# Hybrid decoder step: cache tiles kept together in pairs on TensorE, batched norm sums, idle products in the norms

## The chip, the cores and the metric

The kernel runs on one NeuronCore of one Trainium2 chip. The metric is the device time of one execution in microseconds (us). Three runs of the kernel before took 1901.42, 1902.14 and 1903.34 us, median 1902.14 us. The profiled execution took 1903.54 us, of which 1901.8 us lie between its first and last instruction (the span).

## What is computed

Two layers of a decoder trunk for two request groups that share weights: one prompt of 256 tokens, and 8 samples of 4 tokens each, so 288 columns in all, 1024 channels. Per layer:

```python
h = rmsnorm(x);  proj = h @ w_in                 # one combined input projection
#  A. gated DeltaNet, 8 heads:  q, k = l2norm(q), l2norm(k);  chunked delta rule
#  B. dilated window attention, 3 groups x 4 heads; a sample reads cache_win{1,2,3}_k / _v
#  C. Mamba-2 SSD, 16 heads, gated, grouped RMSNorm
merged = g_dn*(o_dn @ w_br_dn) + g_dil*(o_dil @ w_br_dil) + g_ssm*(o_ssm @ w_br_ssm)
x = x + rmsnorm(merged @ w_out)                  # "mixpost"
x = x + rmsnorm(crossattn(rmsnorm(x)) @ w_mo)    # "mempost"; memory k, v from rmsnorm(mem)
x = x + rmsnorm(relu(rmsnorm(x) @ w_ff1)**2 @ w_ff2)   # "ffnpost"
```

All results are float32. The states of all three mixers are returned as well.

## The kernel before, in words

**Projections.** Activations lie transposed, as eight tiles of 128 channels x 288 columns. Each is split into a high and a low part (`xh`, `xl`), each weight too (`wh`, `wl`), so a 128 x 128 weight tile costs three matmuls of 288 columns into a bank `mmps` (or `mmx`). Weights come from `in_wst` in blocks of four tiles (256 KB, tile `wr`), ScalarE casts `wh`, VectorE subtracts to `wl`. There are 3600 weight tiles, 10,800 such matmuls.

**Background work.** The three mixers, apart from their projections, are Python generators (`spawn`, `step`). At every fourth weight tile, `w` calls `tick`, which advances two of them to their next `yield`. So the program text of the mixers is woven into that of the projections.

**Order on the engines.** The program text is not the final order. A planner at compile time lists each engine's instructions by when it believes their inputs and buffers are there. An instruction that it believes late is put behind later text that is ready. It sets the order once; on the chip each engine runs its list in order, and each instruction waits by semaphore. Buffers come from pools with a fixed number of slots (`N_A` = 50 activation tiles, `N_M` = 9 large tiles `M`, 5 PSUM banks `X`); a load waits until its tile has a slot.

**The cache work of the sample.** `dil_sample` (L1692 on) reads cache tiles of 512 KB (`kc`, from pool `M`) through `caches(name, n, depth=2)`, which loads two ahead. Per layer there are 4, 8 and 2 tiles of keys (`k1`, `k2`, `k3`) and 4, 2 and 8 of values (`v1`, `v3`, `v2`). `qk_cache` (L1667) multiplies key tiles into `sqk`, `pv_cache` (L1676) value tiles into `spo`; each matmul uses 32 of the array's columns, four heads side by side. A float32 matmul stands in the trace as two records, so a tile of values gives 16. `qk_cache` yields after every tile of `k1` and `k3` and every second one of `k2`, `pv_cache` after every second tile. The cross-attention (`cross_sample`, tiles `mqk`, `mpo`) uses the same two helpers with depth 5.

**Sums of squares.** `dn_mix` (L837) forms the norms of q and k per half of the heads: four squares of q on ScalarE, four (eight records of 288 columns) matmuls into `l2` (in the trace: `l`), then the same for k. `mem_norm` (L631) adds eight squares on VectorE (`gather`) and sums the result with four matmuls into `ss`; `ssm_gate` (L1501) adds two squares for each of four groups and sums with four matmuls into `yn`.

**Post-norms.** `postnorm` (L586) runs eight projections, sums the squares (`ss`), forms the factor on VectorE (`row`, nine dependent instructions ending with `rms`), spreads it with four matmuls (`bc`) and updates x, from which the next `xh`, `xl` come. For `mixpost` two pieces of other projection work (`fill`: columns of the memory's keys) stand around the spread; for `mempost` and `ffnpost` nothing does.

Of the kernel before, what the change touches and what calls it, by code (L numbers as in the profile page):

```python
# [10 lines left out]
BF16 = mybir.dt.bfloat16  # L11
I32 = mybir.dt.int32
AF = mybir.ActivationFunctionType
ALU = mybir.AluOpType
# [3 lines left out]
P = 128  # L18
# [8 lines left out]
NSTEP = 2  # L27
IDLE, IDLE2 = 1, 1
GATE = 3
HDV = 1  # L30
RAW, AHEAD = 6, 2
N_A, N_M = 50, 9
# [192 lines left out]
class Net:  # L225
    def __init__(self, ctx, tc, ins, outs, coff, nl):
        self.tc, self.nc = tc, tc.nc
        self.I, self.O, self.nl = ins, outs, nl
        self.coff, self.moff = coff
        pool = lambda name, bufs, **k: ctx.enter_context(tc.tile_pool(name=name, bufs=bufs, **k))  # L230
        self.cpool = pool("cpool", 1)
        self.pa = pool("pa", N_A)
        self.pm = pool("pm", N_M)
        self.pw = pool("pw", 3)
        self.psm = pool("psm", 2)
        self.pr = pool("pr", 1)
        self.mm = pool("mm", 3, space=PSUM)
        self.mx = pool("mx", 5, space=PSUM)
        self.pd = ctx.enter_context(tc.tile_pool(name="pd", bufs=2, space=bass.MemoryType.DRAM))
        self.cbi = self.zi = 0  # L240
        self.order, self.wt = [], {}
        self.nload = self.nsplit = 0
        self.gate, self.nstep, self.sqs = (0,), NSTEP, []
        self.bg, self.lazy, self.done = [], [], set()
        self.setup()


# [34 lines left out]


    def mmul(self, out, lhsT, rhs, start=True, stop=True):
        self.nc.tensor.matmul(out, lhsT, rhs, start=start, stop=stop)  # L285

    def tp(self, out, in_):
        self.nc.tensor.transpose(out, in_, self.ident)
# [85 lines left out]
    def setup(self):  # L374
        nc = self.nc
        self.prmt = {}
        cw = sum(w for _, w in self.coff.values())
        self.cst = self.cpool.tile([P, cw], F32, tag="cst", name="cst")
        self.xt = [self.A(nm="x") for _ in range(8)]
        self.params(0)  # L380
        for c in range(8):
            self.load(self.xt[c], self.I["x"][:, c, :])
            if c < RAW:
                self.load_weights(c)
            if c == 1:
                self.load(self.cst[:, 0:256], self.I["cst"][:, 0:256])
        self.ident, self.ones = self.C("ident"), self.C("ones")
        self.Z = [self.zeros([P, 1024], f"z{i}") for i in range(2)]
        self.CB = [self.zeros([P, 316], f"cb{i}") for i in range(4)]
        self.cmz = self.zeros([P, 2, 256], "cmz")  # L390
        self.St = {}
        for k, w in (("dst", T), ("sst", T + 128)):
            self.St[k] = self.cpool.tile([P, w], F32R, tag=k, name=k)
            nc.gpsimd.memset(self.St[k].bitcast(F32), 0.0)
        self.z3 = self.cpool.tile([P, 512], F32, tag="z3", name="z3")
        nc.vector.memset(self.z3, 0.0)
        self.tsd = self.cpool.tile([P, P], F32, tag="tsd", name="tsd")
        self.cp(self.tsd, self.z3[:, 0:128])
        self.tok0 = self.zeros([P, 3, 32], "tok0")
        self.mc = self.zeros([P, 8, 32], "mc")  # L400
        self.tT = self.zeros([P, 8, 128], "tT")
        self.t64 = self.zeros([P, 8, 64], "t64")
        self.gtok = self.zeros([P, 6, 3, 24], "gtok")
        self.l2t = self.cpool.tile([P, 3, 2, 4], F32, tag="l2t", name="l2t")
        nc.gpsimd.memset(self.l2t, 1.0)
# [133 lines left out]
                self.mmul(ps[32 * g:32 * g + 32, 0:w], self.ones[:, 0:32], sq[:, w * g:w * g + w],  # L539
                          i == 0, i == len(sqs) - 1)  # L540

    def gather(self, acc, sq, w=T):

        if acc is None:
            return sq
        self.tt(acc[:, 0:w], acc[:, 0:w], sq[:, 0:w], ALU.add)
        return acc

    def sums(self, ss):

        def after(k):
            if k == 7:
                self.sumsq(ss, self.sqs)
                self.sqs = []
        return after

    def row(self, ps, w=72):
        r = self.S(w, "rms")
# [27 lines left out]
    def postnorm(self, gname, wname, xs, each, eps=None, fill=None, part=None, k0=0):  # L586

        ss = self.X("ss")
        fs, sqs = [], [None]
        ps = self.projs([(wname, n * 128) for n in range(2)], xs) if k0 == 0 else []  # L590
        for n in range(8):
            b = ps[n] if n < len(ps) else self.proj(wname, n * 128, xs, k0)
            sq = self.A(nm="sq")
            if part is None:
                f = self.A(nm="f")
                last = self.act(sq, b[:, 0:T], AF.Square)
                self.ts(f, b[:, 0:T], self.prm(gname, n))
            else:
                f = part[n]
                self.tt(f, f, b[:, 0:T], ALU.add)  # L600
                last = self.act(sq, f, AF.Square)
                self.act(f, f, AF.Copy, scale=self.prm(gname, n))
            fs.append(f)
            if n < 6:
                sqs[0] = self.gather(sqs[0], sq)
            else:
                sqs.append(sq)
        self.gate = (self.nsplit + GATE, last)
        g0 = self.nsplit + GATE
        self.sumsq(ss, sqs)  # L610
        if eps is None:
            r = self.row(ss)
        else:
            v, r, y, t = self.S(72, "qv"), self.S(72, "rms"), self.S(72, "ry", I32), self.S(72, "rt")
            self.stt(v, ss[:, 0:72], 1.0 / 1024, eps, ALU.mult, ALU.add)
            self.last = self.rsqrt_of(r, v, y, t)
        self.gate = (g0, last, self.last)
        if fill:
            fill[0]()
        bc = self.spread(r)  # L620
        if fill:
            fill[1]()
        res = []
        each = each()
        for n in range(8):
            self.tt(fs[n], fs[n], bc[:, 0:T])
            self.tt(self.xt[n], self.xt[n], fs[n], ALU.add)
            res.append(each(n))
        return res


    def mem_norm(self):
# [2 lines left out]
            self.load(mem[i], self.I["mem"][:, 4 * i:4 * i + 4, :])  # L635
        for _ in range(4):
            yield
        acc = None
        for c in range(8):
            sq = self.A(nm="sq")  # L640
            self.act(sq[:, 0:256], mem[c // 4][:, c % 4], AF.Square)
            acc = self.gather(acc, sq, 256)
            if c % 2:
                yield
        yield
        yield
        ss = self.X("ss")
        self.sumsq(ss, [acc], w=64)
        r = self.row(ss, 64)
        yield  # L650
        yield
# [187 lines left out]
    def dn_mix(self, hf, q, k, v):  # L839
# [2 lines left out]
            yield  # L842

        l2 = self.X("l2")
        for i, src in enumerate((q, k)):
            sqs = [self.A(nm="sq") for _ in range(4)]
            for h in range(4):
                self.act(sqs[h], src[h], AF.Square)
                if h == 1:
                    yield  # L850
            yield 1
            for h in range(4):
                self.mmul(l2[32 * h:32 * h + 32, 0:T], self.C("zs")[:, 31 - i:63 - i], sqs[h], i == 0, i == 1)
        lr = self.A(nm="l2r")
        self.cp(lr, l2[:, 0:T])

# [643 lines left out]

    def ssm_gate(self, xs):  # L1501
        Y = self.Y
        accs = [None] * 4
        for t in range(8):
            z = self.gate_z(IN_OFF["ssz"] + t * 128, xs)
            self.need(f"ssm{t // 2}")
            self.stt(Y[t], Y[t], 0.5, z)
            sq = self.A(nm="sq")
            self.act(sq, Y[t], AF.Square)
            accs[t // 2] = self.gather(accs[t // 2], sq)  # L1510
        yn = self.X("yn")
        for g in range(4):
            self.mmul(yn[32 * g:32 * g + 32, 0:T], self.ones[:, 0:32], accs[g])
        self.ssmR = self.quad_rows(yn, 1.0 / 256)

    def ssm_out(self):
# [125 lines left out]
            self.cp(self.diag(z, h), ps[:, 32 * h:32 * h + 32].rearrange("p (b s) -> p b s", b=NB))  # L1642
        return z.rearrange("p (h b s) -> p h b s", h=4, b=NB)

    def caches(self, name, n, depth=2):

        l, buf = self.l, []

# [14 lines left out]
    def qk_cache(self, ps, qm, tiles, n, nk, per):  # L1663
        for i, t in enumerate(tiles):
            kv = t.rearrange("p (b h k) -> p b h k", b=per, h=4)
            for j in range(per):
                b = i * per + j  # L1667
                for h in range(4):
                    self.mmul(ps[32 * h:32 * h + 32, 0:nk], qm[:, h, b], kv[:, j, h], b == 0, b == NB - 1)
            if i % 2 or per > 1:  # L1670
                yield

    def pv_cache(self, po, tiles, n, prods, first=False, last=False):

        for i, vt in enumerate(tiles):
            pr = prods(i)  # L1676
            for j, (lh, o) in enumerate(pr):
                for h in range(4):
                    self.mmul(po[32 * h:32 * h + 32, 0:128], lh(h), vt[:, o + h * 128:o + h * 128 + 128],
                              first and i + j == 0, last and i == n - 1 and j == len(pr) - 1)  # L1680
            if i % 2:
                yield

    def dil_sample(self):
# [309 lines left out]

    def run(self):
        self.l = 0
        x0, n = [], AHEAD + 1
        with self.tc.manual_schedule(engines={mybir.EngineType.Activation, mybir.EngineType.DVE}):
            for c in range(n):
# [62 lines left out]
```

## Time and profile before

| | us |
|---|---|
| median of 3 runs | 1902.14 |
| the profiled execution | 1903.54 |
| its span | 1901.8 |
| TensorE (PE) busy in the span | 1848.5 (97%) |
| VectorE (DVE) busy | 1411.0 (74%) |
| ScalarE (ACT) busy | 1126.7 (59%) |
| GpSimd (POOL) busy | 305.0 (16%) |
| mean granted TensorE clock | 0.989 of full |

A matmul's duration in the trace holds its way through the array, so the records of a dense stream overlap. What a matmul costs in a stream is the distance between two starts: 0.13 us for 288 columns at full clock. What a visit of other work between two projection matmuls costs is read from ends: the end of the first projection matmul after it, less the end of the last before it, less 0.13 us.

### The profile page before, as it was taken

How to read it: one execution, taken by the hardware profiler on the slowest of the kernel's cores; microseconds unless marked ns; L12 is line 12 of the kernel's file. 1: busy time of each engine (PE TensorE's matmuls, PEld its weight loads, DVE VectorE, ACT ScalarE, POOL GpSimd, SP SyncE). 2: the span in 40 equal slices, each digit the busy share in tenths (PEclk: the TensorE clock that was granted, in tenths of full speed). 3: DMA queues.
4: the chain of work that ended last, by engine and by line, in shares of the span. 5: the costliest groups of instructions: out<-in, count | busy, mean ns of one | idle time of the engine just before them, and what ended most of it. 6: DMA issues, size and time to landing. Idle time of an engine off the chain costs nothing. (4 is left out here: it accounts for less than half of the span.)

```text
span 1901.8 us, 44052 instructions
## 1 busy us (share of the span) xinstructions
PE 1848.5 (97%) x16182; PEld 1726.9 (91%) x16182; DVE 1411.0 (74%) x3168; ACT 1126.7 (59%) x2735; POOL 305.0 (16%) x777
## 2 busy tenths in 40 slices
PE   8999999999999999999899999999999999999997
PEld 8998999988998988999899889989889999789997
DVE  6978767677978758766588785776788887587665
ACT  5666665655555556756466756656554555476563
POOL 3523212322000000000024222133210000000000
PEclk9999999999999999999999999999999999989999
DMA  7545436588554684766555453465875556747763
GB/s 254 174 143 170 118 115 199 161 286 270 188 170 143 208 279 129 242 206 201 153 150 182 123 182 106 142 191 158 303 247 191 172 165 208 246 139 238 212 192 99
DMA packets 184441, 354.49 MB, mean 186 GB/s; under 512 B 30688, under 2 KB 42144, under 8 KB 184224
## 3 DMA queue, kind: packets, MB, share of 16 engines
q1 hardware_dynamic: 176320, 326.44, 55.0%
q0 software_dynamic: 7904, 25.23, 3.9%
q8 instruction: 127, 2.08, 0.4%
q14 instruction: 90, 0.74, 0.1%
HBM read 316.54 MB, written 35.05 MB: 185 GB/s over the span
## 5 line engine op out<-in xcount | busy, mean ns | idle before, releaser
L293 ACT CAST wh<-wr 128x512 fp32r<-128x512 f32 x900 | 555.6, 620 | 563.4 <-PE mmps L285 473.4
L302 DVE TENSOR_TENSOR wl<-wr,wh 128x512 fp32r<-128x512 f32 x900 | 619.7, 692 | 286.3 <-ACT wh L293 273.6
L285 PE MATMUL mmps<-xh,wh 128*128 128x288 f32 x2400 | 728.2, 306 | 14.2 <-ACT wh L293 6.8
L285 PE MATMUL mmps<-xl,wh 128*128 128x288 f32 x2400 | 714.6, 298 | 0.0
L285 PE MATMUL mmps<-xh,wl 128*128 128x288 f32 x2400 | 712.8, 297 | 1.0 <-DVE wl L302 1.0
L285 PEld LDWEIGHTS mmps<-xh,wh 128*128 128x128 f32 x2400 | 453.4, 190 | 33.4 <-issue 12.4
L285 PEld LDWEIGHTS mmps<-xl,wh 128*128 128x128 f32 x2400 | 456.1, 190 | 9.3 <-issue 5.6
L285 PEld LDWEIGHTS mmps<-xh,wl 128*128 128x128 f32 x2400 | 454.7, 189 | 7.7 <-issue 3.8
L285 PE MATMUL mmps<-prs,wh 128*128 128x288 f32 x1280 | 262.8, 298 | 2.9 <-ACT prs L293 2.2
L285 PEld LDWEIGHTS mmps<-prs,wh 128*128 128x128 f32 x1280 | 206.2, 189 | 6.1 <-ACT prs L293 3.0
L285 PE MATMUL mmps<-prs,wl 128*128 128x288 f32 x640 | 189.0, 295 | 0.0
L311 DVE SCALAR_TENSOR_TENSOR cy<-cb,cwh,cy 128x312 f32<-128x312 f32 x240 | 129.4, 539 | 19.3 <-ACT cy L290 12.7
L285 PEld LDWEIGHTS mmps<-prs,wl 128*128 128x128 f32 x640 | 121.0, 189 | 0.0
L285 PE MATMUL mmps<-ph,wh 128*128 128x288 f32 x256 | 76.5, 299 | 0.0
L285 PE MATMUL mmps<-pl,wh 128*128 128x288 f32 x256 | 75.6, 295 | 0.0
L285 PE MATMUL mmps<-ph,wl 128*128 128x288 f32 x256 | 75.6, 295 | 0.0
L330 POOL DMA_DIRECT2D out_osd<-dnu x32 | 17.3, 541 | 346.4 <-DVE dnu L311 338.0
L299 POOL COPY cvp<-cb 128x3 f32<-128x3 f32 x80 | 30.2, 378 | 213.7 <-ACT cb L293 213.4
L290 ACT ACTIVATE ct<-cy 128x312 f32<-128x312 f32 x80 | 37.3, 466 | 37.4 <-DVE cy L311 33.5
L285 PEld LDWEIGHTS mmps<-ph,wh 128*128 128x128 f32 x256 | 48.1, 188 | 2.1 <-ACT b L293 0.8
L285 PEld LDWEIGHTS mmps<-pl,wh 128*128 128x128 f32 x256 | 48.2, 188 | 0.7 <-issue 0.4
L285 PEld LDWEIGHTS mmps<-ph,wl 128*128 128x128 f32 x256 | 48.1, 188 | 0.4 <-issue 0.4
(506 smaller groups left out, 2910.1 us busy)
## 6 DMA issues: line engine op xcount, KB each, us to landing
wr<-in_wst SPq DMA_DIRECT2D x900, 256.0 KB
kc<-in_k SPq DMA_DIRECT2D x28, 512.0 KB
kc<-in_v SPq DMA_DIRECT2D x28, 512.0 KB
dns<-in_dns SPq DMA_DIRECT2D x16, 512.0 KB
h<-in_h SPq DMA_DIRECT2D x16, 512.0 KB
out_oss<-h POOLq DMA_DIRECT2D x16, 512.0 KB, 3.9
kc<-in_km SPq DMA_DIRECT2D x16, 512.0 KB
kc<-in_vm SPq DMA_DIRECT2D x16, 512.0 KB
```

The source lines that it names most:

```text
L285: self.nc.tensor.matmul(out, lhsT, rhs, start=start, stop=stop)
L290: return self.nc.scalar.activation(out, in_, func, **k)
L293: self.nc.scalar.copy(out, in_)
L299: self.nc.gpsimd.tensor_copy(out, in_)
L302: self.nc.vector.tensor_tensor(out, a, b, op=op)
L311: return self.nc.vector.scalar_tensor_tensor(out, a, s, b, op0=op0, op1=op1)
L330: self.nc.gpsimd.dma_start(out=out, in_=in_)
```

## The change

It (1) moves the matmuls of two cache tiles into one step, keeps them behind each other on TensorE, and keeps the next matmul of the program text behind them (`pin`, with `keep_in_program_order`, which adds an edge to the engine's previous instruction in the text); (2) loads three cache tiles ahead in place of two; (3) forms q's and k's sums in one batch of eight matmuls, pinned in the same way; (4) sums the memory's eight squares, and the last group's two in `ssm_gate`, on TensorE alone; (5) adds products of a tile of zeros that nobody reads: 16 at the start, 19 before and 14 behind the spread of each post-norm that has no `fill`.

```diff
+WARM = 16, 19, 14
     def mmul(self, out, lhsT, rhs, start=True, stop=True):
-        self.nc.tensor.matmul(out, lhsT, rhs, start=start, stop=stop)
+        ins = self.nc.tensor.matmul(out, lhsT, rhs, start=start, stop=stop)
+        if self.pin:
+            self.tc.keep_in_program_order(ins)
+            self.pin = self.pin & 2
     def setup(self):
+        self.wz = self.cpool.tile([P, 256], BF16, tag="wz", name="wz")
+        nc.vector.memset(self.wz, 0.0)
+    def warm(self, n):
+        ps = self.X("warm")
+        for _ in range(n):
+            self.mmul(ps[:, 0:256], self.wz[:, 0:128], self.wz)
     def postnorm(...):
-        if fill:
-            fill[0]()
+        fill = fill or [lambda n=n: self.warm(n) for n in WARM[1:]]
+        fill[0]()
         bc = self.spread(r)
-        if fill:
-            fill[1]()
+        fill[1]()
     def mem_norm(self):
-        acc = None
+        sqs = []
         for c in range(8):
-            sq = self.A(nm="sq")
-            self.act(sq[:, 0:256], mem[c // 4][:, c % 4], AF.Square)
-            acc = self.gather(acc, sq, 256)
+            sqs.append(self.A(nm="sq"))
+            self.act(sqs[c][:, 0:256], mem[c // 4][:, c % 4], AF.Square)
             if c % 2:
                 yield
         yield
-        yield
         ss = self.X("ss")
-        self.sumsq(ss, [acc], w=64)
+        self.sumsq(ss, sqs, w=64)
     def dn_mix(...):
         l2 = self.X("l2")
+        sqs = []
         for i, src in enumerate((q, k)):
-            sqs = [self.A(nm="sq") for _ in range(4)]
             for h in range(4):
-                self.act(sqs[h], src[h], AF.Square)
+                sqs.append(self.A(nm="sq"))
+                self.act(sqs[-1], src[h], AF.Square)
                 if h == 1:
                     yield
             yield 1
-            for h in range(4):
-                self.mmul(l2[32 * h:32 * h + 32, 0:T], self.C("zs")[:, 31 - i:63 - i], sqs[h], i == 0, i == 1)
+        for i, sq in enumerate(sqs):
+            self.mmul(l2[32 * (i % 4):32 * (i % 4) + 32, 0:T], self.C("zs")[:, 31 - i // 4:63 - i // 4], sq,
+                      i < 4, i >= 4)
+            self.pin = 2
+        self.pin = 1
     def ssm_gate(self, xs):
-            accs[t // 2] = self.gather(accs[t // 2], sq)
+            if t < 6:
+                accs[t // 2] = self.gather(accs[t // 2], sq)
+            else:
+                last.append(sq)
-    def caches(self, name, n, depth=2):
+    def caches(self, name, n, depth=3):
     def qk_cache(self, ps, qm, tiles, n, nk, per):
         for i, t in enumerate(tiles):
+            self.pin = 2 if i % 2 else 0
             ...
-            if i % 2 or per > 1:
+            if i % 2:
+                self.pin = 1
                 yield
     def pv_cache(...):
+            self.pin = 2 if i % 2 else 0
             ...
             if i % 2:
+                self.pin = 1
                 yield
     def run(self):
         self.l = 0
+        self.warm(WARM[0])
```

## Rows read from the trace of the kernel before

**Rows 1.** The page, section 1: each engine's busy time and share.
```profile
PE 1848.5 (97%) x16182; PEld 1726.9 (91%) x16182; DVE 1411.0 (74%) x3168; ACT 1126.7 (59%) x2735; POOL 305.0 (16%) x777
```

**Rows 2.** Waits: who waited for whom, us in total, times, longest.
```profile
PE bc L285 <- DVE rms L311: 10.3, 4, 2.6
PE mpo L285 <- DMA kc<-in_vm: 4.4, 4, 1.6
PEld sqk L285 <- issue: 4.0, 24, 0.2
```

**Rows 3.** Timeline, PE, mempost of layers 0 and 1: start, us, work, [idle before].
```profile
728.12 1.28 PE L285 MATMUL bc<-rms,cst 128*128 128x72 f32 x8 [2.62 <-DVE rms L311]
731.33 1.09 PE L285 MATMUL mmps<-xh,wh 128*128 128x288 f32 x3 [1.93 <-DVE xh L306]
...
733.38 0.44 PE L285 MATMUL mmps<-xh,wl 128*128 128x288 f32 x1
733.62 0.44 PE L285 MATMUL mmps<-xl,wh 128*128 128x288 f32 x1
...
1671.89 1.95 PE L285 MATMUL bc<-rms,cst 128*128 128x72 f32 x8 [2.62 <-DVE rms L311]
```

**Rows 4.** Windows: length, engines' busy us, granted clock, DMA share and GB/s.
```profile
728.00:736.00 8.00, 5.95 (x27) 5.30 (x28) 6.87 (x17) 2.67 (x7) 0.00 (x0) 0.57 0.21 68
...
947.00:954.30 7.30, 5.37 (x24) 4.69 (x24) 6.32 (x17) 2.57 (x6) 2.69 (x5) 0.53 0.45 155
1594.00:1602.00 8.00, 7.63 (x67) 7.08 (x59) 7.69 (x22) 4.11 (x10) 0.00 (x0) 1.00 0.43 144
...
1671.00:1681.20 10.20, 7.38 (x30) 6.73 (x31) 7.80 (x21) 3.16 (x7) 0.00 (x0) 0.50 0.16 53
```

**Rows 5.** Timeline, PE, mixpost of layer 1, with its fill around the spread.
```profile
1596.63 0.28 PE L285 MATMUL mmps<-ml,wh 128*128 128x256 f32 x1
1596.75 0.28 PE L285 MATMUL mmps<-mh,wl 128*128 128x256 f32 x1
1596.87 1.01 PE L285 MATMUL bc<-rms,cst 128*128 128x72 f32 x8
```

**Rows 6.** Timeline, the first matmul of the kernel and the second low weight part.
```profile
5.34 0.61 PE L285 MATMUL mmps<-xh,wh 128*128 128x288 f32 x1 [5.34 <-ACT wh L293]
...
7.34 0.69 DVE L302 TENSOR_TENSOR wl<-wr,wh 128x512 fp32r<-128x512 f32 x1 [0.90 <-ACT wh L293]
```

**Rows 7.** Timeline, PE, first visit of a value tile in layer 0.
```profile
420.91 0.29 PE L285 MATMUL mmps<-xh,wh 128*128 128x288 f32 x1
421.13 0.64 PE L285 MATMUL spo<-kc,z 128*32 128x128 f32 x16
421.70 0.40 PE L285 MATMUL mmps<-xl,wh 128*128 128x288 f32 x1
```

**Rows 8.** Timeline, PE, last visit of value tiles, and eight more.
```profile
450.36 0.64 PE L285 MATMUL spo<-kc,z 128*32 128x128 f32 x16
450.82 0.40 PE L285 MATMUL spo<-vst,spn 96*32 96x128 f32 x8
```

**Rows 9.** Windows, as rows 4, over the stretch of the value tiles.
```profile
440.00:450.00 10.00, 10.00 (x130) 8.35 (x119) 6.31 (x11) 4.33 (x10) 1.94 (x6) 1.00 0.98 337
```

**Rows 10.** Timeline, PE and ACT, norms of q and k, layer 0.
```profile
122.19 0.69 PE L285 MATMUL l<-sq,cst 128*32 128x288 f32 x8
127.92 0.68 PE L285 MATMUL l<-sq,cst 128*32 128x288 f32 x4
130.05 0.67 PE L285 MATMUL l<-sq,cst 128*32 128x288 f32 x2
...
128.88 0.78 ACT L290 ACTIVATE sq<-k 128x288 f32<-128x288 f32 x2
```

**Rows 11.** Timeline, PE: sums of squares, 64 records and 8.
```profile
22.11 1.21 PE L285 MATMUL ss<-sq,cst 128*32 128x72 f32 x64
...
1531.31 0.32 PE L285 MATMUL ss<-sq,cst 128*32 128x64 f32 x8
```

More of the change, by code (lines that the diff above doesn't have):

```diff
@@ L244, in __init__ @@
         self.bg, self.lazy, self.done = [], [], set()
+        self.pin = 0
         self.setup()
@@ L540, in sumsq, with gather @@
                           i == 0, i == len(sqs) - 1)
-    def gather(self, acc, sq, w=T):
+    def gather(self, acc, sq):
         if acc is None:
             return sq
-        self.tt(acc[:, 0:w], acc[:, 0:w], sq[:, 0:w], ALU.add)
+        self.tt(acc, acc, sq, ALU.add)
         return acc
@@ L1502, in ssm_gate @@
         Y = self.Y
-        accs = [None] * 4
+        accs, last = [None] * 4, []
         for t in range(8):
@@ L1509, in ssm_gate @@
             self.act(sq, Y[t], AF.Square)
-            accs[t // 2] = self.gather(accs[t // 2], sq)
+            if t < 6:
+                accs[t // 2] = self.gather(accs[t // 2], sq)
+            else:
+                last.append(sq)
         yn = self.X("yn")
-        for g in range(4):
-            self.mmul(yn[32 * g:32 * g + 32, 0:T], self.ones[:, 0:32], accs[g])
+        for g, sqs in enumerate([[a] for a in accs[0:3]] + [last]):
+            for i, sq in enumerate(sqs):
+                self.mmul(yn[32 * g:32 * g + 32, 0:T], self.ones[:, 0:32], sq, i == 0, i == len(sqs) - 1)
         self.ssmR = self.quad_rows(yn, 1.0 / 256)
```

## The prediction

> **What bounds the kernel now.** I read the page's busy times first: TensorE works 97% of the span, the next engine 74% [rows 1]. So a microsecond taken from another engine is worth nothing by itself; what counts is time that TensorE spends idle, at the lower clock, or on the way into and out of small work. The view of the waits comes second, because it names the few places where TensorE does stand still: the spread of a post-norm's factor waits four times, 10.3 us in all, for the factor from VectorE, and the cross-attention's value tiles (`mpo`) wait 4.4 us for their loads [rows 2]. No other tile of the caches is named as waited for by a matmul.
>
> Third, the timeline around such a post-norm. TensorE is idle for 2.62 us ahead of `bc` and for 1.93 us behind it, until the first new `xh` is there; after that the matmuls of 288 columns start 0.24 us apart [rows 3]. Fourth, the windows over the same stretch: the granted clock is 0.57, 0.53 and 0.50 of full behind three of the post-norms, and 1.00 behind `mixpost`, where other projection work stands around the spread [rows 4]. With 0.132 us as the full-clock distance of such matmuls and 0.24 us here, the stretches run at 1.2 in place of 2.4 GHz.
>
> Fifth, the timeline where the sample's caches are worked on. One value tile is a visit of its own: the projection matmul before it ends at 420.91 + 0.29 = 421.20, the first one after it at 421.70 + 0.40 = 422.10, so the visit costs 0.90 - 0.13 = 0.77 us [rows 7], of which the sixteen records take far less than all. TensorE is never idle there, but it pays the way in and out once per tile.
>
> **The change part by part.**
>
> *Idle products in the post-norms.* Their price is not in the trace; the nearest row is a projection of 256 columns, 0.117 us apart (0.12 between two starts) [rows 5], so 19 cost 2.2 us and 14 cost 1.6 us. Both fit into idle time that is there anyway, 2.62 and 1.93 us [rows 3]. If that cover is gone (the planner lists them elsewhere), 33 of them cost 3.9 us a post-norm. What they bring is the clock. The stretch of 728 to 736 us has 27 records, 8 of `bc`, 2 of `ss` and 17 of the projection, of which 15 are 0.24 apart; the second post-norm has 14, the third 19 (30 records less 8, 2 and one at full speed) [rows 4]. That is 48 x (0.240 - 0.132) = 5.2 us. The spread itself takes 1.28 us and, in layer 1, 1.95 us, against 1.01 us at full clock [rows 3, 5]: 0.3 + 0.3 + 0.9 = 1.5 us. Sum 6.7 us. VectorE could be late next, since it makes `xl`; behind `mixpost` the same chain feeds TensorE at clock 1.00 with 7.63 of 8.00 us busy [rows 4], so I take the whole sum, with bounds 3 and 8. The fourth post-norm ends the kernel, with no projection behind it: nothing. The third of these drops was the longest; another execution may have drawn a shorter one.
>
> *Sixteen products at the start.* They run while TensorE has nothing until 5.34 us. The first block's twelve matmuls could gain 12 x 0.108 = 1.3 us, but the second block's low part is only made from 7.34 to 8.03 us [rows 6], so I take 0.5, bounds 0 and 1.3.
>
> *Pairs of cache tiles.* A visit of 24 records lasts 450.82 + 0.40 - 450.36 = 0.86 us where one of 16 lasts 0.64 [rows 8]: eight more records cost 0.22, sixteen 0.44. A pair together costs 0.77 + 0.44 = 1.21 us against 1.54 for two visits: 0.33 saved. The value tiles of a layer come in 14 visits, the first of them in rows 7, the last in rows 8; the key tiles in 13 or so (24 entries for both layers in the waits view, rows 2, and two first visits that come without idle time). 27 visits become 14: 13 x 0.33 = 4.3 us a layer, 8.6 in all. The edge, however, only forbids overtaking by the next matmul of the text. Where that is a mixer's, as the code has it for about half of the value pairs (`ssm_mix` is the next generator), projections may still slip between two tiles. I take three quarters, 6.5 us.
>
> Against this stands a new wait. Now the projection behind a pair, and all that TensorE has queued behind it, waits until both tiles have landed; before, projections were let ahead. A pair with four weight tiles behind it needs 1.21 + 12 x 0.132 = 2.8 us on TensorE and moves 2 x 0.52 + 0.26 = 1.3 MB; where the DMA share is 0.98 it moves 337 GB/s [rows 9], so 3.9 us: a wait of up to 1.1 us a pair, 28 pairs, 31 us. The other end is nothing, as TensorE does not wait for these tiles now [rows 2]. I take the value of the nearest case, the cross-attention's 4.4 us [rows 2], because the loads lie further ahead than a pair and key tiles come where the DMA queues have room. Net gain 2.1 us, bounds -22 and +8.6. The third tile ahead is a load earlier in the text; it still needs one of nine slots, so I give it nothing of its own. It is issued by SP, where a load that waits for a slot could hold weights back; there are six weight blocks in flight, so nothing.
>
> The Trainium skill's page "TensorE: Matmul & The Clock Gate", section "Part 2: What happens when you issue a matmul", says that matmuls stay in program order and that only weight loads are pulled ahead. By that rule a late tile stops every projection behind it, and the larger wait holds; rows 2 show such a stop only at `mpo`.
>
> *One batch for q and k.* In the first half of the heads, the visits are 8, 4, 2 and 2 records, each about 0.8 us by the same reading (a visit of 8 lasts 0.69, one of 2 0.67 us); in the second half 8 and 8. Six visits, 4.9 us a layer, become two of 16, each 0.82 + 0.3 = 1.1: 2.6 us saved. But the last two squares of k end at 128.88 + 0.78 = 129.66, 1.7 us behind the first visit for k at 127.92 [rows 10], and projections now wait for them in that half: 0 to 1.7 us. I take 1.1: 1.5 a layer, 3.0 in all, bounds 0 (four more tiles held could make the squares later) and 5.2.
>
> *Sums on TensorE alone.* `mem_norm` gets 64 records in place of 8: 1.21 - 0.32 = 0.9 us a layer, 1.8 in all [rows 11], bounds 0 and 3. The adds that it saves VectorE are off the path. In `ssm_gate` two more records follow an add fewer; nothing.
>
> **Sum.** 6.7 + 0.5 + 2.1 + 3.0 - 1.8 = 10.5 us from the profiled execution's 1903.5, 1893.0. The median of the runs stands 1.4 lower than that execution, so 1891.6 us.
>
> **The rivals.** *A, slower: the caches stop TensorE.* One mechanism, at the pairs of `dil_sample`: the projection pinned behind a pair waits for the second tile. All else brings 6.7 + 0.5 + 8.6 + 3.0 - 1.8 = 17 us, so it decides from 0.6 us a pair on; at 1.1 us the time is 1902 + 14 = 1916. For it: DMA share 0.98 [rows 9]. Against it: no wait there now, and half of the value pairs don't pin a projection.
>
> *B, the idle products stand in the wrong place.* They depend on nothing but a bank, so the planner may use them to fill holes that it believes in, ahead of the norm. Then the clock still falls (6.7 us lost) and up to 4 x 3.9 = 15 us are added; with half of that 1891.6 + 6.7 + 7.7 = 1906, with a quarter 1902. Against it: it sees the same idle time in the norm.
>
> *C, the pairs stay apart.* The edge keeps order, not neighbourhood. Then the pairs bring nothing and cost nothing: 1894, and 1897 if q and k gain nothing either.
>
> *D, all of it works without a wait:* 6.7 + 1.3 + 8.6 + 5.2 - 1.8 = 20 us, 1882.
>
> **How the numbers follow.** Forecast 0.55 (1886 to 1897), A 0.10, B 0.12, C 0.15, D 0.08. The range of 1881 to 1902 holds the forecast, C and D, and the mild end of A and B. A measurement of this kernel tells about 0.2% (3.8 us) from no change. Faster by more: the forecast, C, D and a little of A and B, 0.79; within: 0.11; slower: 0.10.
>
> **What would show it.** Right: a granted clock of 1.00 in the windows behind `mempost` and `ffnpost`, with products named `warm` in both gaps and projections 0.13 us apart from the first `xh`; some 14 visits of `spo` and `sqk` a layer in place of 27, each with both tiles' records; `l` in one visit of 16. Wrong: `spo`, `sqk` or `l` named in the waits as held by a load or by `sq`, or `warm` among the projections. If the time lies above 1898 with the clock held, the pins have cost more than the pairs gave.

## The result and the profile after

| | before | after |
|---|---|---|
| median of the runs, us | 1901.78 (4 runs) | 1913.72 (4 runs) |
| ratio to before | | 1.0065, 95% interval 1.0047 to 1.0082 |
| profiled execution, us | 1903.54 | 1913.91 |
| its span, us | 1901.8 | 1912.1 |
| mean granted TensorE clock | 0.989 | 0.992 |

The changed kernel is 12 us slower, although the clock stands higher on the mean. The forecast was 1891.6 us, with a range of 1881 to 1902: wrong in sign. The time is near the 1916 of rival A, the one in which the caches stop TensorE; how far rival A was right is said below.

The page, section 1, of the changed kernel, against [rows 1]: TensorE is busy 16 us longer with 264 more records; VectorE, ScalarE and GpSimd are within 1 us of before.

```profile
PE 1864.5 (98%) x16446; PEld 1740.5 (91%) x16446; DVE 1410.0 (74%) x3153; ACT 1127.3 (59%) x2735; POOL 304.6 (16%) x777
```

The waits of TensorE after (who waited for whom, us in total, times, longest), against [rows 2]:

```profile
PE sqk L287 <- DMA kc<-in_k: 8.8, 2, 4.6
PE mpo L287 <- DMA kc<-in_vm: 5.3, 6, 2.3
PE spo L287 <- ACT z L298: 3.5, 2, 1.8
...
PE bc L287 <- DVE rms L316: 2.9, 4, 1.0
...
PE l L287 <- ACT sq L295: 1.8, 3, 0.8
```

The wait of `bc` fell from 10.3 to 2.9 us, as forecast. In its place stand waits that the kernel before did not have: 8.8 us for key tiles, 3.5 us of the value matmuls for `z`, 1.8 us of `l` for `sq`. The first two stand at the caches' matmuls, but the wait for `z` (a masked tile that ScalarE writes) is not one for a load; what made it was not followed up. The value matmuls' own waits for loads are small, 1.5 us in all.

The windows after (length; busy us of PE, PEld, DVE, ACT, POOL; granted clock; DMA share; GB/s). The last three lie behind the spreads of the first three post-norms, as those of [rows 4] do; the two ahead of them are in the dilated attention and the cross-attention of layer 0:

```profile
394.00:401.00 7.00, 6.20 (x37) 3.85 (x38) 1.49 (x4) 1.32 (x3) 0.00 (x0) 0.51 0.40 152
711.00:719.00 8.00, 7.01 (x46) 5.17 (x47) 1.20 (x3) 0.74 (x2) 0.00 (x0) 0.57 0.48 182
736.00:744.00 8.00, 7.33 (x56) 6.65 (x57) 8.00 (x21) 4.04 (x9) 0.00 (x0) 1.00 0.22 68
952.80:960.80 8.00, 7.60 (x58) 6.91 (x59) 7.91 (x20) 4.37 (x10) 2.79 (x6) 1.00 0.46 150
1685.00:1695.20 10.20, 9.71 (x74) 9.03 (x75) 9.89 (x26) 6.02 (x14) 0.00 (x0) 1.00 0.17 51
```

Behind the norms the clock is 1.00 where it was 0.57, 0.53 and 0.50. But it is at half behind a cache wait (0.51 from 394 us) and in the cross-attention (0.57 from 711 us), where in the kernel before it was full:

```profile
390.00:400.00 10.00, 10.00 (x87) 8.64 (x80) 9.47 (x22) 5.73 (x13) 1.09 (x4) 1.00 0.79 269
...
700.00:710.00 10.00, 8.36 (x146) 6.11 (x144) 2.42 (x5) 2.96 (x6) 0.53 (x1) 1.00 0.85 286
```

The timeline of TensorE around the first post-norm after, against [rows 3]: the idle products fill both gaps.

```profile
733.71 2.14 PE L287 MATMUL warm<-wz 128*128 128x256 bf16 x18
736.27 1.11 PE L287 MATMUL bc<-rms,cst 128*128 128x72 f32 x8 [0.42 <-DVE rms L316]
737.22 1.69 PE L287 MATMUL warm<-wz 128*128 128x256 bf16 x14
739.31 0.66 PE L287 MATMUL mmps<-xh,wh 128*128 128x288 f32 x3 [0.40 <-DVE xh L311]
```

And the timeline of TensorE at the third pair of `k2` tiles in layer 0:

```profile
389.42 0.64 PE L287 MATMUL sqk<-kc,z 128*32 128x256 f32 x8
389.99 0.53 PE L287 MATMUL qbc<-ql,selr 128*128 128x288 f32 x2
394.80 1.08 PE L287 MATMUL sqk<-kc,z 128*32 128x256 f32 x8 [4.28 <-DMA kc<-in_k]
...
396.22 0.44 PE L287 MATMUL mmps<-xl,wh 128*128 128x288 f32 x1
396.46 0.44 PE L287 MATMUL mmps<-xh,wl 128*128 128x288 f32 x1
```

The first tile of the pair is worked on at 389.42. From 390.52 us TensorE stands for 4.28 us until the second is there, and the projections behind it run 0.24 us apart, at half clock. Layer 1 has the same stop (4.56 us).

SyncE's (SP's) DMA queue over the same time: its timeline, its waits from 374 to 394 us, and of these the ones from 390 us on:

```profile
382.65 8.31 SPq L332 DMA_DIRECT2D wr<-in_wst  x5
391.05 1.33 SPq L332 DMA_DIRECT2D kc<-in_k  x3
```
```profile
SPq L332 <- DVE wl L307: 10.5, 7, 2.5
SPq L332 <- PE sqk L287: 1.8, 1, 1.8
```
```profile
SPq L332 <- DVE wl L307: 2.5, 1, 2.5
```

The load for the late tile is issued at 391.05 us, 0.5 us after TensorE has begun to wait, behind five weight loads; another 3.7 us pass until the tile is there. From 374 to 394 us SP waited 10.5 us for `wl`, which frees a weight buffer, and 1.8 us for `sqk`, which frees a cache buffer. From 390 us on there is one wait only, that of the last weight load for `wl`; the three cache loads behind it leave one after the other with no wait of their own. So at that time it was the weight load, and not a cache buffer, that held them; whether their buffers had been free for long, these rows don't say. The weight loads go as TensorE gets through weights, so the load of a tile cannot run far ahead of the projections that stand next to it in the text.

### The profile page after: what moved, and what is told of

Its sections match the earlier page's. It is cut to its first block, busy times and chain, and to the rows that moved or that the text cites. A ratio compares the mean times of both kernels' runs of the same rounds, so it can differ in the third digit from the quotient of the medians.

```text
span 1912.1 us, 44615 instructions
## 1 busy us (share of the span) xinstructions
PE 1864.5 (98%) x16446; PEld 1740.5 (91%) x16446; DVE 1410.0 (74%) x3153; ACT 1127.3 (59%) x2735; POOL 304.6 (16%) x777
```

## The experiments

All were timed beside the kernel before, whose medians there were 1903.5 to 1903.9 us. None of them leaves out a part of the computation.

### The four parts, each alone

**The cache pairs alone.** Edit to the kernel before:

```diff
+    pin / keep_in_program_order in mmul, qk_cache, pv_cache (as in the change)
-            if i % 2 or per > 1:
+            if i % 2:
+                self.pin = 1
                 yield
-    def caches(self, name, n, depth=2):
+    def caches(self, name, n, depth=3):
```

> The kernel before with the cache pairs alone (pairs in one step, pins, three tiles ahead), nothing else of the change. Theory: the pins are the whole loss. In the changed kernel TensorE waits 8.8 us for the second key tile of a pair and 5 us for value tiles, and the clock falls to half behind the key wait and at `mpo`; by parts of the trace that is 8.3 us in layer 0, about 8 in layer 1 and 3.4 and 2.8 in the cross-attentions: +20 to +23 us, 1922 to 1925. Rival: the clock falls at `mpo` come from another part of the change (time shifted by the norms or by q and k), and the pairs cost their waits alone: +8 to +14, 1910 to 1916. By the prediction the pairs gain 2 us, 1900.

Measured: 1926.31 us, ratio 1.0119 (1.0104 to 1.0135): +22.8 us. The theory held (1.3 us above its range, within the spread of the runs). Its waits:

```profile
PE sqk L286 <- DMA kc<-in_k: 9.0, 2, 4.6
PE mpo L286 <- DMA kc<-in_vm: 8.8, 6, 2.7
...
PE spo L286 <- ACT z L297: 3.5, 2, 1.7
```

9.0 + 3.5 + (8.8 - 4.4 that were there before) = 16.9 us are waits. The other 6 us are put down to the lower clock behind them (the mean granted clock is 0.983, before 0.989), less what fewer visits save; the two were not measured apart.

**The idle products alone.**

```diff
+WARM = 16, 19, 14
-        if fill:
-            fill[0]()
+        fill = fill or [lambda n=n: self.warm(n) for n in WARM[1:]]
+        fill[0]()
         bc = self.spread(r)
-        if fill:
-            fill[1]()
+        fill[1]()
+        self.warm(WARM[0])      (in run, ahead of the first block)
```

> The kernel before with the idle products alone (16 at the start, 19 and 14 around the spread in four post-norms). Theory, as predicted: the clock stays at full behind three post-norms, 6.7 us, and 0.5 to 0.8 at the start: 1894 to 1895, granted clock 1.00 in the 8 us from each spread on. Rival: keeping TensorE busy in the norm only moves the fall of the clock to the cross-attention ahead of it, as the changed kernel shows at 711 and 1660 us: a gain of 2 us or less, 1900 to 1902.

Measured: 1894.38 us, ratio 0.9947 (0.9930 to 0.9964): -9.2 us. The theory held. Behind the spreads at mempost of both layers the clock is 1.00 in the windows (ffnpost of layer 0 likewise), and the cross-attention ahead of them shows no fall:

```profile
727.00:735.00 8.00, 7.34 (x56) 6.66 (x57) 8.00 (x21) 4.04 (x9) 0.00 (x0) 1.00 0.21 66
...
1668.00:1678.00 10.00, 9.60 (x73) 8.96 (x71) 9.68 (x26) 7.35 (x16) 0.00 (x0) 1.00 0.19 58
```

**The batch of q and k alone** (with its pins).

```diff
+        sqs = []
         for i, src in enumerate((q, k)):
-            sqs = [self.A(nm="sq") for _ in range(4)]
...
-            for h in range(4):
-                self.mmul(l2[32 * h:32 * h + 32, 0:T], ..., sqs[h], i == 0, i == 1)
+        for i, sq in enumerate(sqs):
+            self.mmul(l2[32 * (i % 4):32 * (i % 4) + 32, 0:T], ..., sq, i < 4, i >= 4)
+            self.pin = 2
```

> The kernel before with q's and k's sums in one pinned batch alone. Theory: TensorE stands inside the batch while ScalarE makes k's squares (the batch lasts 2.5 and 3.3 us in the changed kernel), so it costs what it saves or more: 0 to +3, 1902 to 1905, with waits of `l` for `sq` of 1 to 2 us in the trace. Rival, the prediction: two visits in place of six gain 3 us, 1899.

Measured: 1906.87 us, ratio 1.0018 (1.0007 to 1.0029): +3.3 us. Slower, as the theory had it, 2 us above its range; the waits are there (`l` for `sq` 1.6 us). Whether the pins make them is tried below.

**The sums on TensorE alone.**

```diff
-            acc = self.gather(acc, sq, 256)
...
-        self.sumsq(ss, [acc], w=64)
+        self.sumsq(ss, sqs, w=64)
```

(and the last group of `ssm_gate`, as in the change)

> The kernel before with the sums of mem_norm (and of the last group in ssm_gate) on TensorE alone. Theory: the adds that VectorE is spared stood between its updates of `y` and `prs`, for which TensorE waited (idle time of 2.6 us from 577 to 588 us in layer 0, and 2.4 us with a fall of the clock from 1518.9 us in layer 1); so it gains 2 us in layer 0 and 3 in layer 1: 1897. Rival, the prediction: the adds are off the path and 128 more records cost 1.8 us, 1904.

Measured: 1899.61 us, ratio 0.9975 (0.9966 to 0.9984): -3.9 us. The sign and most of the gain came as the theory had it, the prediction's +1.8 fell. But the theory's reason is not what the rows show. The kernel before at this place, TensorE, VectorE and ScalarE:

```profile
577.70 0.79 PE L285 MATMUL qbc<-ql,selr 128*128 128x288 f32 x4 [0.82 <-DVE ql L311]
579.58 0.40 PE L285 MATMUL mmps<-prs,wh 128*128 128x288 f32 x1 [1.09 <-ACT prs L293]
...
578.13 0.94 DVE L311 SCALAR_TENSOR_TENSOR y<-y,prm,qbc 128x288 f32<-128x288 f32 x2 [0.49 <-PE qbc L285]
578.99 0.42 DVE L302 TENSOR_TENSOR sq<-sq 128x256 f32<-128x256 f32 x1
...
579.09 1.21 ACT L293 CAST prs<-y 128x288 fp32r<-128x288 f32 x3
```

And TensorE in this kernel:

```profile
578.82 0.79 PE L285 MATMUL qbc<-ql,selr 128*128 128x288 f32 x4
579.54 0.65 PE L285 MATMUL ss<-sq,cst 128*32 128x64 f32 x32
580.48 0.40 PE L285 MATMUL mmps<-prs,wh 128*128 128x288 f32 x1 [0.28 <-ACT prs L293]
```

Before, TensorE waits 1.09 us for the first `prs`, which ScalarE casts from 579.09 us on, behind VectorE's first two `y`. The first add (`sq<-sq`, 0.42 us) comes behind these `y`, so it did not delay that wait. In this kernel the way from `qbc` to `prs` is nearly as long (1.66 us from start to start, before 1.88), but 32 of the 64 records of `ss` stand in it: what was idle time now pays for half of the new records. The wait of 0.82 us ahead of `qbc` is gone as well, with more projections listed ahead of it, and so are two shorter ones behind `prs` (0.23 and 0.40 us). Layer 1 has the same picture (waits of 0.58 and 1.10 us before, 0.30 us in this kernel, `ss` in the gap). Whether the spared adds, the squares that are ready earlier for TensorE, or the `yield` that the edit takes out of `mem_norm` moved these places in the list was not told apart; nor was the part of `ssm_gate`.

The four parts sum to 22.8 - 9.2 + 3.3 - 3.9 = 13.0 us; the whole change measured 11.9.

### What in the pairs costs

**No pins.** The step with two tiles and the third load ahead stay.

```diff
-            self.pin = 2 if i % 2 else 0
-                self.pin = 1
```

> The cache pairs without any pin: two tiles of matmuls in one step of the program text and three loads ahead, the planner free to order as it believes. The pairs alone stood 22.8 us above the kernel before. Theory, the pins: without them the waits for `kc` at `sqk` and `mpo` are gone, 1901 to 1906. Rival, the steps and loads: it is the order of the text (fewer yields, loads further ahead that stand between weights in SP's queue) that makes TensorE reach a tile before its load; then most of the loss stays, above 1915.

Measured: 1901.32 us, ratio 0.9992 (0.9983 to 1.0000). The pins are the loss.

**A pin inside the pair alone.**

```diff
             if i % 2:
-                self.pin = 1
+                self.pin = 0
                 yield
```

> The cache pairs with the second tile kept behind the first, but the next matmul of the text not kept behind the pair. Theory: the loss comes from the work that is kept behind the second tile, so projections go ahead of a pair and the wait at `sqk` (4.6 us in the pairs alone) is gone, 1898 to 1906, at best with the 4 to 6 us that fewer visits save. Rival: keeping tile two behind tile one in itself makes the stop, since what the planner lists after tile two waits with it: 1915 or more.

Measured: 1902.07 us, ratio 0.9993 (0.9983 to 1.0003), 24 us below the pairs with all pins. The one edge from the pair to the next matmul of the text is the whole loss. The pin inside the pair did nothing at all: by tile and shape, TensorE's 16182 records stand in the same order in the traces with it and without any pin. TensorE's timeline of the pair that stopped it, and SP's queue beside it:

```profile
388.56 0.64 PE L286 MATMUL sqk<-kc,z 128*32 128x256 f32 x8
...
395.01 0.64 PE L286 MATMUL sqk<-kc,z 128*32 128x256 f32 x8
```
```profile
390.19 5.86 SPq L331 DMA_DIRECT2D kc<-in_k  x5
```

The load is no earlier (390.19 us, 1.6 us behind the first tile's matmuls, as in the changed kernel), but it is not waited for: the planner lists projections between the two tiles. So this pair stays apart, as rival C had it; the second pair of `k1` and the first two of `k2` stand together. The value tiles all stay apart, in lone visits such as these:

```profile
418.69 0.64 PE L286 MATMUL spo<-kc,z 128*32 128x128 f32 x16
421.99 0.64 PE L286 MATMUL spo<-kc,z 128*32 128x128 f32 x16
```

Fourteen tiles are worked on in 31 us, one per 2.2 us. With all pins, in the changed kernel, the fourteen tiles of a layer make 11 visits: three of the seven pairs stand together, and four stay apart even there. The prediction counted on 7, at three quarters of the saving.

**Pins in the dilated attention alone.**

```diff
-        yield from self.qk_cache(pss, qm, pre, 8, 256, 1)
+        yield from self.qk_cache(pss, qm, pre, 8, 256, 1, keep=False)
...                                    (pv_cache of cross_sample likewise)
-            self.pin = 2 if i % 2 else 0
+            self.pin = 2 if i % 2 and keep else 0
```

> The cache pairs with pins in the dilated attention alone; the cross-attention's tiles as in the kernel before. Theory: 5.7 and 4.1 us of the loss lie at `mpo` and `mo` of the two cross-attentions, which the prediction left out, and go: 1914 to 1918, with no fall of the clock at `mpo`. Rival: the waits at `mpo` follow from loads that come later, not from pins there: 1923 or more.

Measured: 1917.06 us, ratio 1.0075 (1.0062 to 1.0087), 9.2 us below the pairs with all pins. So 9.2 us of the 22.8 lie in the two cross-attentions. Its wait for `mpo` is 2.5 us where all pins had 8.8.

**Five and two tiles ahead** in place of three, all pins:

```diff
-    def caches(self, name, n, depth=3):
+    def caches(self, name, n, depth=5):
```

> The cache pairs with all pins and five tiles loaded ahead in place of three in the dilated attention. Theory: the late key tile stands in SP's queue behind five weight loads (382.7 to 390.9 us in the changed kernel) that wait for TensorE; two tiles further ahead in the text, it is issued before them, so the waits of 4.6 and 4.4 us at `sqk` and the fall of the clock behind them go: 1914 to 1919, the cross-attention's part staying. Rival: the nine slots hold no tile more, so the loads wait for slots and hold weights back: 1926 or more.

Measured: 1921.06 us, ratio 1.0088 (1.0073 to 1.0103). In the right direction, but 2 us short: the wait at `sqk` fell from 9.0 to 6.3 us only.

> The cache pairs with all pins, two tiles loaded ahead as in the kernel before (three in the change, five in an earlier run: 1926.3 and 1921.1 us). Theory: each tile that a load stands earlier in the text shortens the stop of TensorE, so with two it is longer: 1930 to 1945, with waits at `sqk` and `spo` in most pairs. Rival: the loads are issued when slots come free, whatever the text says: 1924 to 1928.

Measured: 1932.37 us, ratio 1.0143 (1.0122 to 1.0164), `sqk` waits 12.9 us. The time came as the theory had it, though TensorE stops at `sqk` five times and not in most pairs: from two over three to five tiles ahead, 1932.4, 1926.3 and 1921.1 us. A longer lead shortens the stop and does not end it.

**The loads issued by ScalarE.**

```diff
-                self.load(t, self.I[name][l, i])
+                self.nc.scalar.dma_start(out=t, in_=self.I[name][l, i])
```

> The cache pairs with all pins (1926.3 us), the cache tiles' loads issued by ScalarE in place of SP. Theory: the late key tile stands in SP's queue behind weight loads that wait for TensorE's progress, which the pin stops; issued elsewhere it comes 3 us or more earlier, and the waits at `sqk` of 9 us shrink by half or more: 1910 to 1919. Rival: slots or the transfer itself are what is late, so the waits stay: 1923 to 1930, or more where ScalarE is held by a load that waits for a slot.

Measured: 1958.28 us, ratio 1.0288 (1.0267 to 1.0308). The expectation fell. ScalarE runs its list in order too: the late load stands at 392.11 us there, behind a cast that waited 1.95 us for VectorE.

```profile
392.05 0.43 ACT L297 CAST prs<-ot 128x288 fp32r<-128x288 f32 x1 [1.95 <-DVE ot L315]
392.11 0.82 ACTq L1656 DMA_DIRECT2D kc<-in_k  x2
```

So this run does not tell the weights in SP's queue from the buffers. For the weights stand SP's waits above (10.5 us for `wl`, and no other from 390 us on) and the gain with the lead. The buffers have a part too: with five tiles ahead SP waited 3.3 us for `sqk`, three times, from 374 to 394 us. More weight or cache buffers, which would part the two, were not tried.

### The batch of q and k

**Without pins.**

```diff
-            self.pin = 2
-        self.pin = 1
```

> The batch of q's and k's sums alone, with no pins. Pinned it cost 3.3 us. Theory: the pins make TensorE stand in the batch while k's squares are made; without them projections come between: 1901 to 1904, no waits of `l` for `sq`. Rival: the batch itself costs, by squares that are made later or by four more tiles held: 1906 or more.

Measured: 1906.24 us, ratio 1.0014 (1.0005 to 1.0023): the theory fell, the batch costs nearly as much without pins. TensorE's timeline in the second half of the heads, first this kernel, then the kernel before:

```profile
238.46 1.92 PE L285 MATMUL l<-sq,cst 128*32 128x288 f32 x14
...
240.90 0.67 PE L285 MATMUL l<-sq,cst 128*32 128x288 f32 x2
```
```profile
241.37 0.69 PE L285 MATMUL l<-sq,cst 128*32 128x288 f32 x8
```

Eight records last 0.69 us when four sums, one for each group of 32 columns, stand together. In the batch k's sums are listed as their squares come: 14 records take 1.92 us, and the last two a visit of their own. The batch broke a group that was whole before. By the ends of the matmuls around them these two visits cost 2.9 us, where the two of 8 records before cost 1.6; the first half, 12, 2 and 2 records in place of 8, 4, 2 and 2, saves 0.3. That is 0.9 us a layer more, 1.8 of the 2.4 us that were measured.

**Later in the text**, so that all squares are there.

```diff
             yield 1
+        yield 2
         for i, sq in enumerate(sqs):
```

> The batch of q's and k's sums alone, with no pins, put two turns later in the program text, so that all eight squares are believed ready. Theory: the batch costs because its matmuls are listed singly as the squares come, so that the four groups of 32 columns no longer run side by side (two records of one group 0.27 us apart, where eight of four groups start within 0.29 us); made when all squares are there it stands as 16 records in one visit, and the time is 1900 to 1903. Rival: what costs is that the norms come later for the chain behind them; then later is worse, 1906 to 1910.

Measured: 1904.75 us, ratio 1.0008 (0.9994 to 1.0021), not to be told from before. In the first half the batch now is one visit, as hoped; in the second it is 14 and 2 records as before:

```profile
131.41 1.18 PE L285 MATMUL l<-sq,cst 128*32 128x288 f32 x16
```

That visit costs 1.3 us where the four visits of before cost 3.2. Of these 1.9 us a layer the second half takes 1.2 back (2.9 in place of 1.6). The 0.7 that are left, 1.4 for both layers, do not show in the time, whose interval is -1.1 to +4.0 us; what else it costs was not settled.

### Sizes and a better kernel

**Twice the idle products in the norms.**

```diff
-WARM = 16, 19, 14
+WARM = 16, 38, 28
```

> The idle products alone (1894.4 us) with twice as many in the norms, 38 and 28. Theory: 19 and 14 just fill the gaps; 33 more at 0.11 us are 3.6 us a norm, of which the idle time still left (0.8 us at mempost, 1.4 at ffnpost) hides a part: 2 x 2.8 + 2.2 and 1 at the end, 9 us more, 1903. Rival: the products are listed elsewhere or cost less, and the time stays below 1898.

Measured: 1901.12 us, ratio 0.9988 (0.9977 to 0.9999): 6.7 us above the single count, between the two expectations. The price was right: 37 of them take 4.21 us, 0.11 us each, and no wait is left ahead of `bc`.

```profile
722.46 4.21 PE L286 MATMUL warm<-wz 128*128 128x256 bf16 x37
```

**The changed kernel without the edge to the next matmul.**

```diff
             if i % 2:
-                self.pin = 1
+                self.pin = 0
                 yield
```

> The changed kernel with one edit: the next matmul of the text is not kept behind a pair of cache tiles. Theory: that one edge is the loss; the time falls by the 24 us that it cost with the pairs alone, to 1890 to 1894 (the three gains of 9.2, 3.9 and 1.5 us and the 3.3 us that the batch of q and k costs), below the kernel before. Rival: together with the other parts something else holds TensorE: 1900 or more.

Measured: 1890.36 us, ratio 0.9933 (0.9920 to 0.9945). One edit turns the change from +12 to -13 us.

**Idle products, sums on TensorE, pairs without that edge; q and k as before.**

> The kernel before with three parts: the idle products, the sums of mem_norm and ssm_gate on TensorE, and the cache pairs with the second tile behind the first but no other matmul kept behind the pair. Alone they measured -9.2, -3.9 and -1.5 us against 1903.5. Theory: they act at different places and add up: 1887 to 1891. Rival: a part of each gain was one and the same fall of the clock, counted twice: 1892 to 1896.

Measured: 1887.29 us, ratio 0.9917 (0.9903 to 0.9930), 16.5 us below the kernel before. The parts add up within the spread of the runs (9.2 + 3.9 + 1.5 = 14.6). The 1.5 us of the pairs are not clear of noise alone, and the two other parts without the pairs were not run, so what the pairs bring here is not shown. Its mean granted clock is 0.999. Of the cache tiles it waits at `mpo` alone (2.4 us); the largest of its waits is the one at `sw`, which every kernel here has:

```profile
PE sw L287 <- POOL tsd L304: 3.2, 2, 1.6
```

**The same with the later batch of q and k.**

> The idle products, the sums on TensorE and the cache pairs without the pin on the next matmul (1887.3 us together), with the later batch of q's and k's sums added. Theory: the later batch brings 1 to 3 us also here: 1884.5 to 1886.5. Rival: it brings nothing or costs as it does alone and unmoved: 1887 to 1891.

Measured: 1890.58 us, ratio 0.9930 (0.9913 to 0.9947): the batch brings nothing here either.

## Why the prediction was wrong, by its own steps

| step | forecast, us | measured alone, us |
|---|---|---|
| idle products, norms and start | -7.2 | -9.2 |
| cache pairs, net | -2.1 | +22.8 |
| of it merged visits (pairs without the edge) | -6.5 | -1.5, not clear of noise |
| of it the wait (the edge to the next matmul) | +4.4 | +24 |
| q and k in one batch | -3.0 | +3.3 |
| sums on TensorE | +1.8 | -3.9 |
| sum | -10.5 | +13.0 (whole change: +11.9) |

**The pin's wait** is the step that failed and decided: 4.4 us in the sum, 24 us in the runs (the waits and the lower clock behind them). What failed is how its price was chosen. The prediction had 31 us as the upper end and took 4.4 us, the wait at `mpo` in [rows 2], as the nearest case. But that wait was measured where the planner was free to list projections ahead of a late tile. Such a row says how late the planner let a tile be, not how late tiles are. The reason given with it, that loads lie further ahead than a pair, was not read in the queue: SP's timeline showed, in the kernel before too, a gap of seven weight loads from 378.4 to 391.2 us between two loads of key tiles:

```profile
378.36 12.73 SPq L327 DMA_DIRECT2D wr<-in_wst  x7
391.19 8.49 SPq L327 DMA_DIRECT2D kc<-in_k  x6
```

The prediction asked whether a cache load holds weights back, and gave that nothing; it was the weights that stood ahead of the cache load.

**Rival A** had the mechanism in outline (the work pinned behind a pair waits for its second tile) and the sign, at a chance of 0.10. That its 1916 lies so near 1913.7 is partly luck. Its 31 us were 28 short waits of 1.1 us, where the DMA share is highest. What came was two stops of 4.28 and 4.56 us at key tiles that were issued late, with a DMA share of 0.64 from 389 to 395 us, 3.5 us for `z`, the cross-attentions, and the clock behind the stops. The value tiles, whose stretch gave A its price, waited 1.5 us for loads in all, and its other terms (q and k, the sums, the merged visits) were off both ways.

The page "TensorE: Matmul & The Clock Gate" of the Trainium skill, section "Part 2: What happens when you issue a matmul", has matmuls in program order, and the prediction noted that by it a late tile stops all projections behind it. The traces agree: 4.28 us idle ahead of the second tile of the third `k2` pair, with the projections behind it.

The cross-attention was left out of the step, although it calls the same two helpers: 9.2 us. So was what a wait does beyond itself: the clock falls behind it. The clock's price stood in the same prediction, for the norms, and was not carried over.

**The merged visits** were worked out right for a pair that is together (1.21 us against 1.54). That it would be, for three quarters, was a choice without a row. The trace of before shows lone value visits 1.7 to 3.8 us apart, and of the seven pairs of value tiles three came together, with all pins.

**q and k**: a visit of 16 was put at 1.1 us and measures 1.3 where it happens; in the changed kernel none of the four batches stands together without a stop. The bound of "0 to 1.7 us" for k's late squares held (TensorE stood 1.8 us for `sq` in all), but it was taken as a wait alone, and the loss of the four sums side by side in the second half, 1.2 us a layer, was not seen.

**The sums of mem_norm**: "the adds that it saves VectorE are off the path" was said from the share of 74% in [rows 1]. The term that failed is the price of the records, 1.8 us in full. TensorE has idle time at that place, its waits for `prs` and `ql` (2.2 and 1.4 us), which stood in the view of waits and were not followed back; half of the new records fell into it, and the waits shrank to 0.6 us. That the adds were off the path of the first `prs` was right by the rows above; whether sparing them helped elsewhere is open.

**The idle products** went as worked out: both gaps are filled, 32 of the 33 take 3.8 us (2.14 + 1.69 in the timeline after) of the 4.55 us that the gaps had, and the clock is 1.00 in the three windows. The 2 us by which the gain exceeds the forecast, and the start's part, can't be told from the spread of the runs. Rival B did not occur.

## What to carry to other kernels

An order edge's price is not the wait that the trace shows without it: find when the tile that the pinned work needs is issued and lands, and when the engine would reach it, and remember that behind such a stop the clock may fall too. Where a planner is free to move work, keep it free on the side where the late input is; an edge to the work behind a group can cost all, and one inside the group changed nothing here, because the order was the same without it. Small work added to a busy engine is free where the engine stands idle, so look where the new records will be listed before charging them, and follow each named wait back to the instructions that stood ahead of its releaser.

## What the runs showed of the hardware that was not expected

The clock does not fall behind every stop of the same length. Ahead of `sw` TensorE stands 1.5 to 1.6 us in every kernel here, at the same work. Over six microseconds around the end of this stop the granted clock was 0.72 in layer 0 of the kernel before (first fence) and of the pairs without pins (second fence). In the kernel with a pin inside the pair alone (third fence) it was 1.00 in layer 0 and 0.55 in layer 1:

```profile
182.50:188.50 6.00, 5.53 (x55) 4.98 (x56) 2.59 (x8) 1.75 (x7) 0.89 (x5) 0.72 0.76 265
```
```profile
180.70:186.70 6.00, 4.92 (x51) 4.25 (x51) 2.72 (x5) 1.87 (x8) 1.26 (x5) 0.72 0.84 273
```
```profile
181.00:187.00 6.00, 4.90 (x61) 4.34 (x62) 3.96 (x11) 2.36 (x10) 1.99 (x7) 1.00 0.89 298
1121.50:1127.50 6.00, 4.71 (x30) 4.01 (x34) 2.36 (x4) 2.08 (x9) 1.44 (x6) 0.55 0.78 270
```

The last two kernels have TensorE's records in the same order throughout. So one execution's falls are partly chance, and a fall that a single trace shows should not be booked whole to one edit.

Four sums of float32 squares, one in each group of 32 columns, last 0.69 us together; one alone lasts 0.67 us [rows 10]. Kept together, the other three add almost nothing to the duration.
